# Weight-block sums one half product earlier, and the seven-product stream three half tiles later, in a one-core decoder layer

## The chip, the core and the metric

The kernel runs on one core of a Trainium2 chip. The metric is the device time in microseconds of one execution. Every number of time below is from three timed runs of the kernel before or from one further execution of it under the hardware profiler.

## What is computed

One decoder layer on 256 tokens of width 2048, all in float32. The core of the reference, cut:

```python
proj = x @ w_in
q_a, k_a, v_a, z_a, u_g, v_g, z_g, q_c, z_c, g_logit = jnp.split(proj, split_at, axis=-1)
y_a = _moba_attention(q_a, k_a, v_a) * jax.nn.silu(z_a)
y_g = _spatial_gating(u_g, v_g, w_s, b_s, ln_v_g, ln_v_b) * jax.nn.silu(z_g)
mem_k = mem @ w_mem_k
mem_v = mem @ w_mem_v
y_c = _memory_attention(q_c, mem_k, mem_v) * jax.nn.silu(z_c)
gates = jax.nn.sigmoid(g_logit)
merged = (gates[:, :, 0] * (y_a @ w_branch_attn)
          + gates[:, :, 1] * (y_g @ w_branch_sgu)
          + gates[:, :, 2] * (y_c @ w_branch_mem))
x = _layer_norm(DN_ALPHA * x + merged @ w_out, ln_g, ln_b)
```

## The kernel before

Every operand is kept as two float32r parts, a rounded one (`hi`) and the rest (`lo`), and a product of two float32 matrices is made of three TensorE products: hi by hi, hi by lo, lo by hi. The helper `split` (lines 58 to 60) makes the parts: ScalarE (ACT) copies the source to `hi`, then VectorE (DVE) subtracts it from the source to `lo`. So each weight passes ACT and then DVE before TensorE (PE) can use it.

Two streams of work share the engines.

**The classic stream** works through 112 chunks of weights of 1 MB, each in two halves. `load_chunk` brings chunk 70, say, to the tile `raw70`; `prep_half` splits half 0 to `hi70_0`, `lo70_0` (128x1024); `c_half` hands it to 12 or 16 products. `channel_tile` (16 products a half, alternately 512 and 256 columns wide, lines 187 and 188) makes the projections, and `gated_branch` (12 products of 512 columns, lines 712 to 714) the three branch products. In the order of the program: memory values and keys; zc and qc with the memory attention (`ms`, `mpt`, `mo`); za with branch 2; q and k with eight heads of block attention (`s`, `pt`, `o`); ug with branch 0 (chunks 67 to 74); ug (75 to 79); zg with the spatial gating (`mix`, scales of the tile `vg` on line 663; chunks 80 to 87); branch 1 (88 to 95); the output product. The `hi` and `lo` tiles have 3 buffers each, so a half may be split three halves ahead.

**The seven-product stream** (`s_stream`, lines 327 to 393) makes eight units of 1024 columns (the six gate halves, the attention values and v_g) with seven products of 2x2 blocks instead of eight. A unit has 14 half products, numbered s = 14u + r, two for each of M1, M5, M6, M3, M7, M4, M2 in this order. The weights of unit u come in four blocks with two halves of 1 MB each: the tile `b0_u_h` is B11, `b1` B12, `b2` B22, `b3` B21. M5, M6 and M4 need B11 less another block. These sums are made in place in `b0`, one after another, by `sub` on DVE (128x2048, line 311). A fourth sum, B12 less B22, is made in `b1` in M3.

`s_prep(s)` readies half product s: for M5, M6 and M4 the sum, then the split to `sh<s>` and `sl<s>` (128x2048), then the load of the block whose buffer has just come free. `s_stream` calls `s_prep(s + 2)` behind the 12 products of s. The tag `shl` has 4 buffers, hence two half products of `sh` and `sl`. The block `b3` is loaded behind the split of M3 (`s_load`, line 295) and used by the sum of M4, four half products later; it takes the buffer that the split of M3 frees.

The two streams are interleaved by a loop at the end (lines 776 to 784). After each of the 160 steps of the classic stream behind zc, it takes as many of the 112 half products as keep them in proportion, once `LEAD` steps have passed, so that the last is due `TAIL` steps before the end:

```python
while done_s < S_STEPS and done_s * (C_STEPS - LEAD - TAIL) < (done_c - LEAD) * S_STEPS:
    step(lambda: next(ss))
```

This sets the order in which the program is written down. The framework then arranges the instructions of each engine anew by its own estimate of when each is ready (`schedule_with_timeline_sim=True`), so the order in which the engines get them is not the program's. On the chip each engine takes its list from front to back.

Of the kernel before, what the change touches and what calls it, by code (L numbers as in the profile page):

```python
# [11 lines left out]
ALU = mybir.AluOpType  # L12
# [4 lines left out]
S = 256  # L17
# [10 lines left out]
def decoder_layer(ctx, tc, xT, memT, x_tok, w_st, w_mv, w_mk, w_zc, w_qc, w_za, w_qk, w_ug, w_zg,  # L28
                  w_br, w_o, w_sT, sgu_bc, ln_g, ln_b, out):
    nc = tc.nc  # L30
# [17 lines left out]
    def new_acc(name):  # L48
        return psum.tile([P, 512], F32, tag="acc", name=name, bufs=3)

    def new_sps(name):
        return psum.tile([P, 512], F32, tag="sps", name=name, bufs=3)
# [5 lines left out]
    def split(hi, lo, v):  # L58
        nc.scalar.activation(hi, v, AF.Copy)  # L59
        nc.vector.tensor_tensor(lo, v, hi.bitcast(F32), op=ALU.subtract)  # L60
# [89 lines left out]
    def c_half(ahead=2):  # L150
        while len(ready) < ahead + 1 and ptr["half"] < 2 * len(chunks):
            prep_half()
        return ready.pop(0)
# [31 lines left out]

    def channels_mm(ps, x, hi, lo, first, last):
        nc.tensor.matmul(ps, hi, x, start=first, stop=False)  # L187
        nc.tensor.matmul(ps[:, S:2 * S], lo, x[:, 0:S], start=False, stop=last)

    def channel_tile(xs, name, fin):  # L190

        ps = new_acc(name)
        for h in range(2):
            hi, lo = c_half()
            for k in range(8):
                c = slice(k * P, (k + 1) * P)
                channels_mm(ps, xs(8 * h + k), hi[:, c], lo[:, c], h == 0 and k == 0, h == 1 and k == 7)
            if h == 1:
                def done():
                    fin(ps)  # L200
                    tick()
                late.append(done)
            yield
# [81 lines left out]
    UNITS = 8  # L285
    PRODUCTS = ("M1", "M5", "M6", "M3", "M7", "M4", "M2")
    FORM = {"M5": 1, "M6": 2, "M3": 4, "M7": 3}
    rt, shl, xsf, sp = {}, {}, {}, {}

    def s_load(u, blk, h):  # L290
        if u >= UNITS:
            return
        tag, bufs = ("rA", 2) if blk == 0 else ("rB", 4)
        t = wts.tile([P, 2048], F32, tag=tag, name=f"b{blk}_{u}_{h}", bufs=bufs)
        nc.sync.dma_start(t, w_st[u, blk, h])
        rt[u, blk, h] = t

    B11, B12, B22, B21 = range(4)

    def s_prep(s):  # L300
        u, r = divmod(s, 14)
        if u >= UNITS:
            return
        p, h = divmod(r, 2)
        p = PRODUCTS[p]
        if p in FORM:
            t = wts.tile([P, 4, 2 * P], F32R, tag="xsf", name=f"xf{s}", bufs=3)
            nc.sync.dma_start(t.bitcast(F32), xf_d[FORM[p], h])
            xsf[s] = t
        b = lambda blk: rt[u, blk, h]  # L310
        sub = lambda o, x, y: nc.vector.tensor_tensor(o, x, y, op=ALU.subtract)  # L311
        src = {"M1": B11, "M5": B11, "M6": B11, "M4": B11, "M3": B22, "M7": B12, "M2": B21}[p]
        if p == "M5":
            sub(b(B11), b(B12), b(B11))
        elif p == "M6":
            sub(b(B11), b(B22), b(B11))
        elif p == "M4":
            sub(b(B11), b(B21), b(B11))
        hi = wts.tile([P, 2048], F32R, tag="shl", name=f"sh{s}", bufs=4)
        lo = wts.tile([P, 2048], F32R, tag="shl", name=f"sl{s}", bufs=4)  # L320
        split(hi, lo, b(src))
        shl[s] = (hi, lo)
        if p == "M3":
            sub(b(B12), b(B22), b(B12))
            s_load(u, B21, h)
        elif p == "M7":
            s_load(u + 1, B12, h)
        elif p == "M4":
            s_load(u + 1, B11, h)
        elif p == "M2":  # L330
            s_load(u + 1, B22, h)

    def snap(name):
        return work.tile([P, 512], F32, tag="snap", name=name, bufs=5)

    def s_stream(finish):

        bank, kept = {}, {}

        def keep(name, ps):  # L340
            kept[name] = snap(name)
            nc.scalar.activation(kept[name], ps, AF.Copy)

        def result(u, t, n, ps, name):
            r = kept[name]
            nc.vector.tensor_tensor(r, ps, r, op=ALU.add)
            finish(u, t, n, r)

        def evacuate(u, p):
            if p == "M1":  # L350
                keep(f"k1_{u}", bank["b"])
            elif p == "M5":
                keep(f"k5_{u}", bank["d"])
            elif p == "M6":
                keep(f"k6_{u}", bank["b"])
            elif p == "M3":
                result(u, 0, 1, bank["d"], f"k6_{u}")
            elif p == "M7":
                keep(f"k7_{u}", bank["b"])
                result(u, 1, 1, bank["b"], f"k5_{u}")  # L360
            elif p == "M4":
                result(u, 1, 0, bank["c"], f"k7_{u}")
            else:
                result(u, 0, 0, bank["a"], f"k1_{u}")

        BANK = {"M1": "b", "M6": "b", "M7": "b", "M5": "d", "M3": "d", "M4": "c", "M2": "a"}
        for s in range(14 * UNITS):
            u, r = divmod(s, 14)
            p, h = divmod(r, 2)
            p = PRODUCTS[p]  # L370
            if h == 0 and p in ("M1", "M5", "M4", "M2"):
                bank[BANK[p]] = new_sps(f"s{p}_{u}")
            ps = bank[BANK[p]]
            hi, lo = shl.pop(s)
            for kk in range(4):
                k = 4 * h + kk
                if p in FORM:
                    ah, al = xsf[s][:, kk, 0:P], xsf[s][:, kk, P:2 * P]
                else:
                    k += 0 if p == "M1" else 8  # L380
                    t = P if p == "M4" else 0
                    ah, al = xhl[:, k, t:t + P], xhl[:, k, S + t:S + t + P]
                c = slice(kk * 512, (kk + 1) * 512)
                first = h == 0 and kk == 0 and p in ("M1", "M5", "M4", "M2")
                last = h == 1 and kk == 3
                nc.tensor.matmul(ps, ah, hi[:, c], start=first, stop=False, skip_group_check=True)  # L386
                nc.tensor.matmul(ps, ah, lo[:, c], start=False, stop=False, skip_group_check=True)  # L387
                nc.tensor.matmul(ps, al, hi[:, c], start=False, stop=last, skip_group_check=True)  # L388
            xsf.pop(s, None)
            s_prep(s + 2)  # L390
            if h == 1:
                late.append(lambda u=u, p=p: evacuate(u, p))
            yield
# [76 lines left out]
    while x_work:  # L470
        x_work.pop(0)()
        step(lambda: None)
    s_prep(0)
    s_prep(1)


    yhl = {}
# [281 lines left out]
    def classic():  # L759
        yield from gate_tiles("zc", AF.Silu, szc_d)  # L760
        new_y(2)
        yield from mem_attention()
        yield from gate_tiles("za", AF.Silu, sza_d, range(3))
        yield from gated_branch(2, 0)
        yield from gate_tiles("za", AF.Silu, sza_d, range(3, 8))
        new_y(0)
        yield from block_attention()
        yield from gate_tiles("ug", AF.Gelu_apprx_tanh, gu_d, range(3))
        yield from gated_branch(0, 1)
        yield from gate_tiles("ug", AF.Gelu_apprx_tanh, gu_d, range(3, 8))  # L770
        new_y(1)
        yield from gating()
        yield from gated_branch(1, 2)

    C_STEPS, S_STEPS = 160, 14 * UNITS
    LEAD, TAIL = 2, 14
    cs, ss = classic(), s_stream(s_finish)
    done_c = done_s = 0
    for _ in run(cs):
# [39 lines left out]
    for n in range(3):  # L819
        ps = [new_acc(f"o{n}_{t}") for t in range(2)]  # L820
        for kq in range(8):
            hi, lo = c_half()
# [8 lines left out]
    for t in range(2):  # L831
        for i, c0 in enumerate((1536, 1792)):
            ps = new_sps(f"o{3 + i}_{t}")
# [82 lines left out]
```

## Time and profile before

| | |
|---|---|
| three timed runs | 1009.95, 1011.45, 1011.49 us; median 1011.45 us |
| the profiled execution | 1014.38 us, of it 1012.7 us from its first to its last instruction |
| TensorE's granted clock, mean | 0.99 of full speed |
| DMA | 269.28 MB, 266 GB/s in the mean |

The profiled execution is the one that all rows below come from. It is 2.9 us longer than the median of the timed runs. Busy shares overlap: PE's matmuls are pipelined, and a stretch in which PE is shown busy can still hold fewer products than another of the same length. A lowered clock shows in the granted clock of a stretch.

### The profile page before, as it was taken

What the parts mean: (1) busy time and instruction counts of PE and PEld (TensorE: products, weight loads), DVE (VectorE), ACT (ScalarE), POOL (GpSimd) and SP (SyncE); (2) the same over time, 40 slices, a digit from 0 to 9 for tenths busy, and PEclk for the clock granted to TensorE, in tenths of its full rate; (3) what the DMA queues carried; (4) which work ended last, traced back from release to release, by engine and by line L of the source; (5) the groups of instructions that cost most, each with busy time, mean ns of one, the idle gap of its engine ahead of it and who ended that gap; (6) DMA issues with size and microseconds to landing.
All of it is one profiled execution on the core that took longest, in us unless ns stands there. A gap on an engine that the chain in (4) does not pass through costs nothing.

```text
span 1012.7 us, 12913 instructions
## 1 busy us (share of the span) xinstructions
PE 982.4 (97%) x4888; PEld 826.9 (82%) x4888; DVE 820.6 (81%) x800; ACT 590.6 (58%) x646; POOL 12.0 (1%) x17
## 2 busy tenths in 40 slices
PE   9999899999999999999999999979998999999995
PEld 7788788888888788888888888858877888878885
DVE  5865987898779799888979898899979877676657
ACT  5654665565577566556556566867555559554430
POOL 0000000000000000000000000000000010000000
PEclk9999999999999999999999999989999999999998
DMA  8899589738965897598379648937994785778622
GB/s 330 313 387 414 181 304 348 277 132 296 364 223 168 295 382 278 165 362 346 134 271 356 236 139 281 382 106 269 414 366 147 284 286 183 249 259 303 238 84 83
DMA packets 68126, 269.28 MB, mean 266 GB/s; under 512 B 7521, under 2 KB 21601, under 8 KB 45537
## 3 DMA queue, kind: packets, MB, share of 16 engines
q1 hardware_dynamic: 68064, 268.47, 72.2%
q8 instruction: 38, 0.62, 0.2%
q14 instruction: 24, 0.19, 0.0%
HBM read 245.37 MB, written 23.07 MB: 265 GB/s over the span
## 4 chain that ended last, share of the span: by engine, by line
PE 85%; DVE 5%; ACT 4%; DMA 3%; issue 2%; POOL 0%; SPq 0%; DVEq 0%; ACTq 0%
PE sM L386 9%; PE sM L387 9%; PE sM L388 9%; PE b L713 4%; PE b L714 3%; PE b L712 3%; PE zc L187 3%; PE k L187 3%; PE qc L187 3%; PE za L187 3%; PE q L187 3%; PE mk L187 3%; PE o L800 3%; PE o L799 3%; PE o L798 3%; PE mv L423 3%
## 5 line engine op out<-in xcount | busy, mean ns | idle before, releaser
L59 ACT ACTIVATE hi<-raw 128x1024 fp32r<-128x1024 f32 (+1 forms) x218 | 228.3, 1051 | 191.4 <-PE o L800 29.1
L60 DVE TENSOR_TENSOR lo<-raw,hi 128x1024 fp32r<-128x1024 f32 (+1 forms) x218 | 263.1, 1214 | 77.2 <-ACT hi L59 76.4
L60 DVE TENSOR_TENSOR sl<-b,sh 128x2048 fp32r<-128x2048 f32 x112 | 256.3, 2291 | 57.1 <-ACT sh L59 56.7
L59 ACT ACTIVATE sh<-b 128x2048 fp32r<-128x2048 f32 x112 | 214.4, 1915 | 99.6 <-PE sM L387 89.3
L311 DVE TENSOR_TENSOR b<-b,b 128x2048 f32<-128x2048 f32 x64 | 146.3, 2289 | 8.0 <-DMA b<-in_w_st_dram 7.8
L386 PE MATMUL sM<-sh,xf 128*128 128x512 f32 x256 | 101.3, 396 | 6.5 <-ACT sh L59 6.5
L387 PE MATMUL sM<-sl,xf 128*128 128x512 f32 x256 | 100.6, 393 | 2.5 <-DVE sl L60 2.5
L388 PE MATMUL sM<-sh,xf 128*128 128x512 f32 x256 | 100.2, 391 | 0.0
L387 PE MATMUL sM<-sl,xhl 128*128 128x512 f32 x192 | 76.8, 400 | 0.6 <-DVE sl L60 0.6
L386 PE MATMUL sM<-sh,xhl 128*128 128x512 f32 x192 | 77.4, 403 | 0.0
L713 PE MATMUL b<-lo,yhl 128*128 128x512 f32 x192 | 76.1, 397 | 1.2 <-DVE lo L60 1.2
L388 PE MATMUL sM<-sh,xhl 128*128 128x512 f32 x192 | 76.3, 397 | 0.0
L714 PE MATMUL b<-hi,yhl 128*128 128x512 f32 x192 | 74.9, 394 | 0.0
L712 PE MATMUL b<-hi,yhl 128*128 128x512 f32 x192 | 74.0, 398 | 0.9 <-ACT hi L59 0.9
L386 PEld LDWEIGHTS sM<-sh,xf 128*128 128x128 f32 x256 | 48.3, 189 | 18.3 <-ACT sh L59 7.9
L387 PEld LDWEIGHTS sM<-sl,xf 128*128 128x128 f32 x256 | 48.2, 188 | 12.9 <-DVE sl L60 3.2
L388 PEld LDWEIGHTS sM<-sh,xf 128*128 128x128 f32 x256 | 48.1, 188 | 10.3
L187 PE MATMUL ug<-xhl,hi 128*128 128x512 f32 x128 | 46.3, 400 | 1.5 <-ACT hi L59 1.5
L187 PE MATMUL q<-xhl,hi 128*128 128x512 f32 x128 | 46.5, 399 | 0.0
L187 PE MATMUL qc<-xhl,hi 128*128 128x512 f32 x128 | 46.2, 400 | 0.0
L187 PE MATMUL zc<-xhl,hi 128*128 128x512 f32 x128 | 45.7, 398 | 0.4 <-ACT hi L59 0.4
L187 PE MATMUL k<-xhl,hi 128*128 128x512 f32 x128 | 46.0, 397 | 0.0
(296 smaller groups left out, 1853.1 us busy)
## 6 DMA issues: line engine op xcount, KB each, us to landing
b<-in_w_st_dram SPq DMA_DIRECT2D x64, 1024.0 KB, 7.2
xf<-xf SPq DMA_DIRECT2D x64, 512.0 KB, 6.0
raw<-in_w_br_dram SPq DMA_DIRECT2D x24, 1024.0 KB, 6.8
raw<-in_w_qk_dram SPq DMA_DIRECT2D x16, 1024.0 KB, 7.3
raw<-in_w_o_dram SPq DMA_DIRECT2D x16, 1024.0 KB, 5.4
raw<-in_w_mk_dram SPq DMA_DIRECT2D x8, 1024.0 KB, 10.1
raw<-in_w_zc_dram SPq DMA_DIRECT2D x8, 1024.0 KB, 6.5
raw<-in_w_qc_dram SPq DMA_DIRECT2D x8, 1024.0 KB, 7.6
```

Of the source, the lines that this page charges most:

```text
L59: nc.scalar.activation(hi, v, AF.Copy)
L60: nc.vector.tensor_tensor(lo, v, hi.bitcast(F32), op=ALU.subtract)
L187: nc.tensor.matmul(ps, hi, x, start=first, stop=False)
L311: sub = lambda o, x, y: nc.vector.tensor_tensor(o, x, y, op=ALU.subtract)
L386: nc.tensor.matmul(ps, ah, hi[:, c], start=first, stop=False, skip_group_check=True)
L387: nc.tensor.matmul(ps, ah, lo[:, c], start=False, stop=False, skip_group_check=True)
L388: nc.tensor.matmul(ps, al, hi[:, c], start=False, stop=last, skip_group_check=True)
L423: nc.tensor.matmul(ps[t][n], lhs, rhs[:, n * 512:(n + 1) * 512], start=(k == 0 and rhs is hi and lhs is xh[t]), stop=(k == KT - 1 and lhs ...
L712: nc.tensor.matmul(ps[t], yh, hi[:, c], start=(k == 0), stop=False)
L713: nc.tensor.matmul(ps[t], yh, lo[:, c], start=False, stop=False)
L714: nc.tensor.matmul(ps[t], yl, hi[:, c], start=False, stop=(k == 7))
L798: nc.tensor.matmul(ps[:, 0:n], mh, hi, start=first, stop=False)
```

## The change

The three sums of M5, M6 and M4 leave `s_prep` for a function `s_sum`, which `s_stream` calls with s + 3 just ahead of `s_prep(s + 2)`. So in the program the sum stands one half product ahead of its split. The first one is called with 2 behind `s_prep(1)`. The sum of M3 stays in `s_prep`. LEAD goes from 2 to 5 and TAIL from 14 to 11: the proportion of the two streams between is unchanged (144 steps to 112 half products), and every half product is written three steps of the classic stream later. (`channels_mm` now returns its last product; nothing uses it.)

```diff
+    def s_sum(s):
+
+        u, r = divmod(s, 14)
+        if u >= UNITS:
+            return
+        p, h = divmod(r, 2)
+        other = {"M5": B12, "M6": B22, "M4": B21}.get(PRODUCTS[p])
+        if other is not None:
+            o = rt[u, B11, h]
+            nc.vector.tensor_tensor(o, rt[u, other, h], o, op=ALU.subtract)
+
     def s_prep(s):
...
         src = {"M1": B11, "M5": B11, "M6": B11, "M4": B11, "M3": B22, "M7": B12, "M2": B21}[p]
-        if p == "M5":
-            sub(b(B11), b(B12), b(B11))
-        elif p == "M6":
-            sub(b(B11), b(B22), b(B11))
-        elif p == "M4":
-            sub(b(B11), b(B21), b(B11))
         hi = wts.tile([P, 2048], F32R, tag="shl", name=f"sh{s}", bufs=4)
...
             xsf.pop(s, None)
+            s_sum(s + 3)
             s_prep(s + 2)
...
     s_prep(0)
     s_prep(1)
+    s_sum(2)
...
     C_STEPS, S_STEPS = 160, 14 * UNITS
-    LEAD, TAIL = 2, 14
+    LEAD, TAIL = 5, 11
```

What it does to the engines' lists is shown at three places. In the names the first number is that of the half product (`sh84`, `sl84`), of the chunk and half (`hi70_0`), or of the unit and half (`b0_6_1`); the last number counts tiles and means nothing.

**Place 1: ACT where unit six begins (its first half product is 84).** Before:

```order
L59 ACTIVATE sh84_5606<-b0_6_0_5425 128x2048
L599 ACTIVATE ptT7_5303<-pt7_5299 128x384
L704 ACT_TABLE_LOAD
L704 ACTIVATE sg000_5382<-sg000_5382 128x512
L59 ACTIVATE sh85_5638<-b0_6_1_5462 128x2048
L704 ACTIVATE sg010_5385<-sg010_5385 128x512
L704 ACTIVATE sg001_5523<-sg001_5523 128x512
L753 ACTIVATE vg_5405<-k1_5_5039 128x512
L704 ACTIVATE sg011_5526<-sg011_5526 128x512
L59 ACTIVATE sh86_5720<-b0_6_0_5425 128x2048
L635 ACT_TABLE_LOAD
L635 ACTIVATE vg_5405<-vg_5405 128x512
```

and now, from half product 82 on:

```order
L59 ACTIVATE sh82_5567<-b3_5_0_5281 128x2048
L711 ACT_TABLE_LOAD
L711 ACTIVATE sg000_5340<-sg000_5340 128x512
L711 ACTIVATE sg010_5343<-sg010_5343 128x512
L760 ACTIVATE vg_5459<-k5_5_5228 128x512
L642 ACT_TABLE_LOAD
L642 ACTIVATE vg_5459<-vg_5459 128x512
L59 ACTIVATE sh83_5619<-b3_5_1_5325 128x2048
L59 ACTIVATE hi70_0_5496<-raw70_5389 128x1024
L760 ACTIVATE vg_5459<-k7_5_5550 128x512
L711 ACT_TABLE_LOAD
L711 ACTIVATE sg001_5490<-sg001_5490 128x512
```

Before, the last head (`ptT7`) and the first sigmoids of branch 0 (`sg`) fall between `sh84` and `sh86`, and no chunk is split there: `hi70_0` follows only on `sh87`. Now they fall between `sh82` and `sh84`, and the chunks of branch 0 (`hi70_0`, `hi70_1`, `hi71_0`) alternate with `sh83`, `sh84`, `sh85`. Six instructions stand between `sh82` and `sh83`.

**Place 2: DVE from the split of half product 34 (the first of M3 in unit two) to the sum of M4, which takes `b3_2_0`.** Before:

```order
L60 TENSOR_TENSOR sl34_2869<-b2_2_0_2418,sh34_2868 128x2048
L60 TENSOR_TENSOR lo39_1_2913<-raw39_2773,hi39_1_2912 128x1024
L726 TENSOR_TENSOR sg201_2810<-b2_10_2808,sg201_2810 128x512
L60 TENSOR_TENSOR sl35_2906<-b2_2_1_2511,sh35_2905 128x2048
L726 TENSOR_TENSOR sg211_2813<-b2_11_2809,sg211_2813 128x512
L311 TENSOR_TENSOR b0_2_0_2319<-b3_2_0_2873,b0_2_0_2319 128x2048
L60 TENSOR_TENSOR lo40_0_2963<-raw40_2840,hi40_0_2962 128x1024
```

and now:

```order
L60 TENSOR_TENSOR sl34_2929<-b2_2_0_2515,sh34_2928 128x2048
L60 TENSOR_TENSOR lo40_1_2938<-raw40_2798,hi40_1_2937 128x1024
L60 TENSOR_TENSOR lo41_0_2977<-raw41_2872,hi41_0_2976 128x1024
L60 TENSOR_TENSOR lo41_1_3015<-raw41_2872,hi41_1_3014 128x1024
L309 TENSOR_TENSOR b0_2_0_2399<-b3_2_0_2933,b0_2_0_2399 128x2048
L60 TENSOR_TENSOR sl35_2970<-b2_2_1_2594,sh35_2969 128x2048
```

The sum has come ahead of `sl35`, which now waits behind it.

**Place 3: DVE where unit seven begins, from the split of half product 99 to that of 100.** Before:

```order
L60 TENSOR_TENSOR sl99_6364<-b0_7_1_6164,sh99_6363 128x2048
L311 TENSOR_TENSOR b0_7_0_6122<-b1_7_0_6002,b0_7_0_6122 128x2048
L311 TENSOR_TENSOR b0_7_1_6164<-b1_7_1_6075,b0_7_1_6164 128x2048
L60 TENSOR_TENSOR lo77_0_6084<-raw77_5968,hi77_0_6083 128x1024
L663 TENSOR_TENSOR vg_5405<-vg_5405,sc1_6494 128x2x128
L663 TENSOR_TENSOR vg_5405<-vg_5405,sc2_6601 128x2x128
L60 TENSOR_TENSOR lo77_1_6126<-raw77_5968,hi77_1_6125 128x1024
L208 TENSOR_TENSOR ug4_6166<-ug4_6082,ug4l_6167 128x256
L311 TENSOR_TENSOR b1_7_0_6002<-b2_7_0_6213,b1_7_0_6002 128x2048
L663 TENSOR_TENSOR vg_5405<-vg_5405,sc3_6690 128x2x128
L60 TENSOR_TENSOR sl100_6442<-b0_7_0_6122,sh100_6441 128x2048
```

and now:

```order
L60 TENSOR_TENSOR sl99_6444<-b0_7_1_6240,sh99_6443 128x2048
L60 TENSOR_TENSOR lo82_0_6463<-raw82_6318,hi82_0_6462 128x1024
L60 TENSOR_TENSOR lo82_1_6484<-raw82_6318,hi82_1_6483 128x1024
L208 TENSOR_TENSOR zg1_6528<-zg1_6461,zg1l_6529 128x256
L309 TENSOR_TENSOR b0_7_1_6240<-b1_7_1_6151,b0_7_1_6240 128x2048
L678 TENSOR_TENSOR m0_6536<-mix0_6533,sc0_6360 128x256
L60 TENSOR_TENSOR lo83_0_6551<-raw83_6412,hi83_0_6550 128x1024
L60 TENSOR_TENSOR sl100_6523<-b0_7_0_6194,sh100_6522 128x2048
```

Unit seven stood beside chunks 76 to 79 and the scales of `vg`, and now stands beside chunks 81 to 84; three sums stood between the two splits, and one does now.

## Rows read from the trace of the kernel before

**Rows 1.** The page, part 1: busy time, share of the span, instructions.
```profile
PE 982.4 (97%) x4888; PEld 826.9 (82%) x4888; DVE 820.6 (81%) x800; ACT 590.6 (58%) x646; POOL 12.0 (1%) x17
```

**Rows 2.** Whom PE waited for: us in total, times, longest us.
```profile
PE sM L386 <- ACT sh L59: 6.5, 3, 2.8
PE sM L387 <- DVE sl L60: 3.1, 3, 1.8
PE mix L668 <- POOL ws L657: 1.8, 1, 1.8
PE b L713 <- DVE lo L60: 1.2, 2, 0.8
```

**Rows 3.** Busy us by stretch (x instructions): PE, PEld, DVE, ACT, POOL; clock, DMA share, GB/s.
```profile
75.00:100.00 25.00, 25.00 (x146) 21.86 (x145) 13.29 (x14) 11.90 (x14) 0.00 (x0) 1.00 1.02 418
325.00:350.00 25.00, 25.00 (x112) 20.69 (x111) 18.26 (x14) 15.93 (x15) 0.00 (x0) 1.00 0.78 272
...
655.00:694.00 39.00, 33.80 (x127) 26.07 (x126) 38.02 (x34) 27.67 (x29) 0.00 (x0) 0.87 0.44 150
...
745.00:790.00 45.00, 39.17 (x200) 32.29 (x199) 44.55 (x39) 26.02 (x28) 3.45 (x1) 1.00 0.59 210
```

**Rows 4.** The same columns, two short stretches inside the first loss.
```profile
668.00:672.00 4.00, 4.00 (x12) 3.12 (x12) 4.00 (x3) 1.90 (x3) 0.00 (x0) 0.58 0.00 0
679.00:686.00 7.00, 6.81 (x16) 5.02 (x17) 7.00 (x8) 1.70 (x3) 0.00 (x0) 0.52 0.00 0
```

**Rows 5.** DVE in order of time: start us, us, line, operation.
```profile
665.01 2.29 DVE L60 TENSOR_TENSOR sl<-b,sh 128x2048 fp32r<-128x2048 f32 x1
667.21 2.29 DVE L311 TENSOR_TENSOR b<-b,b 128x2048 f32<-128x2048 f32 x1
669.41 2.29 DVE L60 TENSOR_TENSOR sl<-b,sh 128x2048 fp32r<-128x2048 f32 x1
...
679.27 1.24 DVE L726 TENSOR_TENSOR sg<-b,sg 128x512 f32<-128x512 f32 x2
680.42 2.29 DVE L60 TENSOR_TENSOR sl<-b,sh 128x2048 fp32r<-128x2048 f32 x1
...
689.43 2.36 DVE L60 TENSOR_TENSOR lo<-raw,hi 128x1024 fp32r<-128x1024 f32 x2
691.70 0.17 DVE L217 RECIPROCAL vgr<-vgr 128x2 f32<-128x2 f32 x1
```

**Rows 6.** ACT in order of time, the same columns.
```profile
660.04 1.28 ACT L704 ACT_TABLE_LOAD   x1
...
661.87 1.90 ACT L59 ACTIVATE sh<-b 128x2048 fp32r<-128x2048 f32 x1
663.68 1.14 ACT L704 ACTIVATE sg<-sg 128x512 f32<-128x512 f32 x2
```

**Rows 7.** DVE at the sum of M4 in unit two, in order of time.
```profile
339.12 2.29 DVE L60 TENSOR_TENSOR sl<-b,sh 128x2048 fp32r<-128x2048 f32 x1 [3.71 <-ACT sh L59]
...
348.98 2.29 DVE L311 TENSOR_TENSOR b<-b,b 128x2048 f32<-128x2048 f32 x1 [3.03 <-DMA b<-in_w_st_dram]
351.19 1.22 DVE L60 TENSOR_TENSOR lo<-raw,hi 128x1024 fp32r<-128x1024 f32 x1
```

**Rows 8.** The DMA queue (SP) there: start of the issue.
```profile
341.44 0.33 SPq L295 DMA_DIRECT2D b<-in_w_st_dram  x1
```

**Rows 9.** Line 311 (all sums): DVE's idle time ahead of it, us and times, and what ended it.
```profile
  DMA b<-in_w_st_dram: 7.8, 4
```

**Rows 10.** The page, part 6: loads of blocks, KB each, median us to landing.
```profile
b<-in_w_st_dram SPq DMA_DIRECT2D x64, 1024.0 KB, 7.2
```

**Rows 11.** A split of unit five on DVE, and the first product that takes it.
```profile
619.18 2.28 DVE L60 TENSOR_TENSOR sl<-b,sh 128x2048 fp32r<-128x2048 f32 x1
...
627.49 0.40 PE L387 MATMUL sM<-sl,xf 128*128 128x512 f32 x1
```

**Rows 12.** The chain that ended last, in order of time: start us, us, what.
```profile
859.69 4.41 DMA gl<-k
...
878.21 5.39 DMA sg<-gl
```

More of the change, by code (lines that the diff above doesn't have):

```diff
@@ L187, in channels_mm @@
         nc.tensor.matmul(ps, hi, x, start=first, stop=False)
-        nc.tensor.matmul(ps[:, S:2 * S], lo, x[:, 0:S], start=False, stop=last)
+        return nc.tensor.matmul(ps[:, S:2 * S], lo, x[:, 0:S], start=False, stop=last)
     def channel_tile(xs, name, fin):
```

## The prediction

> **What bounds the kernel now.** Four views, in this order. The page's first part gives TensorE (PE) 982.4 us of 1012.7, 97%, and DVE 820.6 [rows 1]: PE is the engine to look at, and what can be won lies in the places where it runs short. The view of whom PE waited for [rows 2] names them: the split of the seven-product stream on ACT (`sh`, 6.5 us, one wait of 2.8), the same on DVE (`sl`, 3.1 us), once `mix` on POOL (1.8 us), twice a `lo` (1.2 us). Short waits hide here, and so do products that start late while PE counts as busy, so the third view is products per stretch [rows 3]. Where nothing holds PE back, 112 products of 512 columns take 25 us, 0.223 us each; the channel tiles with their alternating widths take 25/146 = 0.171 us. From 655 to 694, 127 products should take 28.3 us and take 39.0: **10.7 us are lost**, with DVE busy for 38.02 of 39.0, PE's granted clock 0.87 and DMA at 0.44. Within it are 668 to 672 with clock 0.58 and 679 to 686 with 0.52 [rows 4], near the lower of the two levels, 1.2 GHz, after PE had run short of weights. From 745 to 790 PE idles for 45.00 - 39.17 = **5.8 us**, and DVE is busy for 44.55 of 45. So DVE, idle for a fifth of the span, is the bound in these two stretches, where units six and seven start. The fourth view, DVE's instructions in time [rows 5], gives prices as start to start: a split or a sum of 128x2048 2.20 us, the split of a half chunk 2.27/2 = 1.13, a 128x512 operation 1.15/2 = 0.57. On ACT [rows 6]: `sh` 1.81, a 128x512 activation 0.57, a table load 1.28.
>
> The cause in both stretches: a half product is 12 products, 2.7 us of PE, and in M5, M6 and M4 it takes 4.4 us of DVE (sum and split). Beside classic halves (2.7 us of PE for 1.13 us of DVE) this averages out; where half products stand back to back, or extra DVE work joins them, it doesn't.
>
> **The change, part by part.**
>
> *The sums' new place.* The number of operations stays the same, so DVE keeps its 820.6 us. The framework arranges the lists anew, and in the order 52 of the 64 sums stand behind the same split as before. What acts is therefore mainly the shift of the two streams against each other. The returned last product costs nothing (no instruction). The first hundred or so rows of DVE's list are the same, so I put the start of the stream at 0.
>
> *Unit six (place 1).* Before, half products 84 to 87 ran almost alone: between `sl84` and `sl87` DVE had 8 large operations, 17.6 us, and 3.2 of small ones, 20.8 in all, for 57 products, 12.7 us: 8.1 short. Now chunks of branch 0 alternate with them: 8 large (17.6), 6 `lo` (6.8), 8 small (4.6), 29.0 us, for 101 products, 22.5 us: 6.5 short. A lead of splits over products covers some of it: `sl77`, in unit five, ends 6.0 us ahead of its product [rows 11]. The shortfall of before came through in full, with 2.6 more from ACT and the rest; so I let 2 be covered and 4.5 remain (ends 0.5 and 6.5). On ACT, between `sh82` and `sh83`, there are two table loads and four activations, 4.8 us, and then `sh83`, 1.8: 6.6 against two halves of PE, 5.4, 1.2 short (0 to 2.8, the longest such wait now). For the collision of the last head with the unit's first blocks I allow 1.8 (0 to 2.8). Sum 7.5 for 10.7: **-3.2** (ends -10.2 and +1.4).
>
> *Unit seven (place 3).* Three sums stood between `sl99` and `sl100`, now one, and the scales of `vg` are gone from there. From `sl98` to `sl101` DVE has 7 large (15.4), 3 `lo` (3.4) and 2 us of small ones, 20.8 us as before, but PE now has 36 products of 512 columns and 50 of channels, 8.0 + 8.6 + 0.7 of mixing = 17.3 for 14.0. 3.5 us short, which a lead of 6.0 covers. `mix` now comes some 12 halves behind the issue of what it waited for; that wait goes. 0.5 of 5.8 remains: **-5.3** (-5.8 to -2.8, if half of the shortfall and the `mix` wait stay).
>
> *The wait on b3 (place 2).* The load of `b3` is issued when the split of M3 ends, 339.12 + 2.29, at 341.44 [rows 7, 8]; the sum of M4 waits 3.03 us for it, starts at 348.98, and the next `lo` only behind it, at 351.19 [rows 7]. All such waits come to 7.8 us in 4 places [rows 9], and the median load takes 7.2 [rows 10]. Now 3 `lo`, 3.4 us, stand between `sl34` and the sum, where 4.5 us stood: the wait becomes about 4.1, and `sl35` stands behind it. It ends 7.5 + 2.2 + 2.2 = 11.9 us after `sl34`, while PE has 34 products, 7.6 us; 4.3 short less a lead of 0.4 to 3: 2.2, of which before had 0.7. **+1.5** (0 to +3.2).
>
> *Behind unit six.* DVE's list stays full into unit seven, so a stall is put off rather than paid once: **+1.5** (0 to +3).
>
> *The end.* The chain of the end goes through the gate's store to DRAM and its reload, 4.41 and 5.39 us [rows 12], and three steps later in the order it lies nearer to its use. **+0.5** (0 to +5.4, one reload).
>
> *Sum:* -3.2 - 5.3 + 1.5 + 1.5 + 0.5 = **-5.0**. The profiled execution took 1014.38 us and would take 1009.4; it stands 2.9 above the median of the timed runs, 1011.45, so for the median I say **1006.4**.
>
> **The rivals.**
>
> *Both stalls vanish.* If the alternation at unit six lets the lead of 6.0 us [rows 11] cover the 6.5 there, PE doesn't run dry and the clock stays at 1.00: -10.7 - 5.8 + 3.5 = -13.0, **998.4**. For it: of 10.7 us, much was products at a lowered clock [rows 4], which go with the cause. Against: the lead must have been built by then, and DVE is loaded from the head before. 0.12.
>
> *The shift only moves the shortfall.* DVE's work is the same, the sums hardly moved, and what was short in unit six turns up in units six and seven: the sum of the gains is paid back, **1011.5**, within 0.2% (2 us, about what a measurement of this kernel tells from no change). For it: DVE full for 38.02 of 39 and 44.55 of 45 us [rows 3], and six us still short. Against: over the span DVE is idle for a fifth [rows 1], so there is room around these stretches to work ahead. This is also the case in which the change doesn't do what it says. 0.16.
>
> *Slower: DVE's list blocks on a load.* A sum of M4 that comes earlier stands earlier in front of a load that doesn't. DVE takes its list in order: at 351.19 a `lo` whose source was ready began only behind the sum that had waited 3.03 us [rows 7]. Counting for all 16 such sums the work between the split of M3 and the sum, the shortfall to 7.2 us was 25.3 in all and is now 33.5: +8.2 us of waits, with splits `sl35`, `sl63` and `sl77` now behind them. It decides wherever the lead of the splits is below the wait, as around `sl34`; where it is 6.0, as at `sl77`, the wait is free. If all 8.2 come through, and half of unit six's gain falls away, -1.6 - 5.3 + 8.2 + 1.5 + 0.5 = +3.3: **1014.8**. The Trainium skill, "PSUM — Partial Sum Buffer", section "Engine vs sequencer instructions", calls the queues of ScalarE, VectorE and GpSimdE strictly first in, first out; by that rule a sum put earlier can only add to the wait of what follows it, and the trace agrees at the one place shown, 351.19. Against this rival: the four waits now total 7.8 us, and PE's waits for `sl` and `lo` together only 4.3 [rows 2, 9]. 0.18.
>
> **How the numbers follow.** Forecast 0.54, both stalls vanish 0.12, moved 0.16, slower 0.18. The range goes from 998.5, where the second case is centred, to 1014.5, just short of the centre of the last; half of each lies outside, 0.15. The forecast's own range, from its unknowns of about 3 us each way, is 1002.5 to 1010. Faster by over 0.2%: 0.54 + 0.12 = 0.66; the same 0.16; slower 0.18.
>
> **What would show it.** Up to the first 117 us nothing should differ. Where unit six starts, right is: about 7 us lost instead of 10.7, a clock above 0.87, and `hi70_0` beside `sh83`. Where unit seven starts: DVE still near 100%, PE idle by less than 1 us, no wait of `mix` on POOL. At the sum of `b0_2_0`: an idle time of 4 us for a DMA, `sl35` behind it, and PE short by some 2 us. DVE's idle time on loads of blocks should grow from 7.8 us toward 10 to 16. The forecast is wrong if PE has a clock near 0.5 in unit six for as long as now, if a new stretch with full DVE and idle PE appears behind unit seven, or if PE's wait for `sl` grows beyond the 3.1 us of now in units two to five, which would be the last rival.

## The result, and the profile after

Five timed runs of the changed kernel give a median of 1004.72 us (1002.88 to 1006.71) beside 1011.45 us: a ratio of 0.9936, 95% interval 0.9918 to 0.9955, so 6.7 us faster; 5.0 were forecast, 1006.4 us. The profiled execution took 1006.01 us (span 1004.3), 1.3 us above its median, and is 8.4 us shorter than the one of before.

The page's part 1 of the changed kernel:

```profile
PE 979.5 (98%) x4888; PEld 824.4 (82%) x4888; DVE 819.6 (82%) x800; ACT 590.5 (59%) x647; POOL 13.2 (1%) x17
```

Against [rows 1] the work is the same and the span shorter. Whom PE waited for (us in total, times, longest):

```profile
PE sM L391 <- ACT sh L59: 4.4, 2, 2.8
PE sM L392 <- DVE sl L60: 2.6, 1, 2.6
PE b L720 <- DVE lo L60: 1.6, 3, 0.8
```

Of the lines of [rows 2], `mix` on POOL is gone. Busy time by stretch, columns as in [rows 3], changed kernel:

```profile
655.00:694.00 39.00, 36.87 (x157) 28.68 (x156) 35.85 (x33) 32.71 (x32) 0.00 (x0) 1.00 0.71 257
694.00:745.00 51.00, 48.04 (x233) 39.54 (x232) 48.40 (x54) 30.09 (x30) 0.00 (x0) 1.00 0.86 310
745.00:790.00 45.00, 45.00 (x234) 38.19 (x233) 40.46 (x31) 30.12 (x30) 3.29 (x3) 1.00 0.81 317
```

and the second of them in the kernel before:

```profile
694.00:745.00 51.00, 51.00 (x234) 42.30 (x232) 43.36 (x40) 28.69 (x24) 0.00 (x0) 1.00 0.98 390
```

From 655 to 694 PE now makes 157 products instead of 127, at a granted clock of 1.00 instead of 0.87; 157 x 0.223 = 35.0 us, so 4.0 are lost where 10.7 were. From 745 to 790 it no longer idles, where 5.8 us were lost. Between the two a new idle time of 3.0 us has appeared.

The whole span can be set out in this way: for each product the time from its start to the next one's, less the median of this time over all products of the same line, tiles and shape; what exceeds 0.06 us is summed. It gives PE's lost time in us. The third and fourth rows are two runs told of below, sums_only and shift_only; all five engines' lists are those of the kernel before in the one, and those of the changed kernel in the other, so that each set of lists is seen in two executions:

| | start to 130 | 130 to 640 | 640 to 694 | 694 to 740 | 740 to 800 | behind 800 | all |
|---|---|---|---|---|---|---|---|
| before | 10.5 | 5.9 | 11.7 | 0.0 | 7.0 | 2.3 | 37.3 |
| changed | 12.5 | 5.7 | 3.9 | 3.8 | 0.2 | 2.8 | 28.9 |
| lists of before (sums_only) | 10.8 | 5.1 | 9.1 | 0.6 | 8.4 | 1.0 | 35.0 |
| changed lists (shift_only) | 9.5 | 5.5 | 4.3 | 4.5 | 0.2 | 0.9 | 24.9 |

From before to changed the sum fell by 8.4 us, the difference of the two spans. The start, whose list did not change, differs by 2.0; the same lists lost 9.5 there in shift_only, so that much is scatter between executions. The other pair shows what is more than scatter: from 740 to 800 the loss goes from 7.0 and 8.4 us to 0.2 in both, while from 640 to 740 it goes from 11.7 and 9.7 to 7.7 and 8.8, so by 4.0 in one pair and by 0.9 in the other. Most of the gain that holds is unit seven's. The lowered clock varies likewise: with the same lists the granted clock from 655 to 694 was 0.87 in the kernel before and 0.96 in sums_only.

DVE in order of time behind unit six's start, changed kernel, and the longest of PE's waits there:

```profile
692.43 2.28 DVE L309 TENSOR_TENSOR b<-b,b 128x2048 f32<-128x2048 f32 x1
694.63 1.22 DVE L60 TENSOR_TENSOR lo<-raw,hi 128x1024 fp32r<-128x1024 f32 x1
695.77 2.28 DVE L322 TENSOR_TENSOR b<-b,b 128x2048 f32<-128x2048 f32 x1
697.97 0.16 DVE L215 TENSOR_SCALAR vgv<-vmv 128x2 f32<-128x2 f32 x1
698.04 2.28 DVE L60 TENSOR_TENSOR sl<-b,sh 128x2048 fp32r<-128x2048 f32 x1
```

```profile
700.38 0.50 PE L392 MATMUL sM<-sl,xf 128*128 128x512 f32 x1 [2.59 <-DVE sl L60]
```

The split at 698.04 is `sl87`. The two sums ahead of it are for half products 88 (M6) and 93 (M7); they stand first in DVE's list, and PE waits 2.59 us for the split behind them.

### The profile page after: what moved, and what is told of

Read it like the earlier page. It is cut to its first block, busy times and chain, and to the rows that moved or that the text cites. A ratio compares the mean times of both kernels' runs of the same rounds, so it can differ in the third digit from the quotient of the medians.

```text
span 1004.3 us, 12911 instructions
## 1 busy us (share of the span) xinstructions
PE 979.5 (98%) x4888; PEld 824.4 (82%) x4888; DVE 819.6 (82%) x800; ACT 590.5 (59%) x647; POOL 13.2 (1%) x17
## 4 chain that ended last, share of the span: by engine, by line
PE 79%; DVE 9%; DMA 6%; issue 3%; ACT 3%; SPq 0%; DVEq 0%; ACTq 0%
PE sM L391 8%; PE sM L392 8%; PE sM L393 8%; PE za L187 3%; PE k L187 3%; PE q L187 3%; PE zg L187 3%; PE qc L187 3%; PE mk L187 3%; PE mv L429 3%; PE o L806 3%; PE o L807 3%; PE o L805 3%; PE zc L187 3%; PE b L720 2%
## 5 line engine op out<-in xcount | busy, mean ns | idle before, releaser
L309 DVE TENSOR_TENSOR b<-b,b 128x2048 f32<-128x2048 f32 x48 | 109.5, 2283 | 15.3 <-DMA b<-in_w_st_dram 15.3
L187 PE MATMUL za<-xhl,hi 128*128 128x512 f32 x128 | 46.2, 400 | 0.0
```

The costliest lines, as they stand in the source:

```text
L309: nc.vector.tensor_tensor(o, rt[u, other, h], o, op=ALU.subtract)
```

## Experiments

"Before" in each is the median of the kernel before, measured beside it.

### Which half of the change acts

sums_only, the changed kernel but for

```diff
-    LEAD, TAIL = 5, 11
+    LEAD, TAIL = 2, 14
```

> The kernel before with the sums written one half product ahead of their split, and the two streams in the proportion of before (LEAD 2, TAIL 14). Theory (only the shift acts): the lists of all five engines are those of the kernel before row for row, so the time is that of before within 0.2% (1009.4 to 1013.5 us) and PE again loses some 10 us from 655 to 694 and 6 us from 745 to 790. Rival (the sums' place brings part of it): faster by 1 to 5 us.

1012.17 us, before 1012.47; ratio 0.9997 (0.9988 to 1.0007). shift_only, the kernel before but for

```diff
-    LEAD, TAIL = 2, 14
+    LEAD, TAIL = 5, 11
```

> The kernel before with LEAD 5 and TAIL 11, the sums left directly ahead of their splits. Theory (only the shift acts): the lists of all five engines are those of the changed kernel, so the time is that of the changed kernel, 1004.7 us within 2 us, and the profile's places of loss are its places. Rival (the sums' place brings part of it): slower than the changed kernel by 1 to 5 us.

1003.56 us, before 1012.47; ratio 0.9919 (0.9906 to 0.9932), the changed kernel's 0.9936 within scatter. With line and tile numbers left out, the lists of all five engines of sums_only are those of the kernel before, row for row, and those of shift_only are the changed kernel's. So the framework undoes the move of the sums altogether, and the change is its two numbers.

### Is it DVE's work that bounds the two stretches?

nosums6 and nosums7 are the kernel before, with the three pairs of sums of one unit left out, here those of unit six (7 stands for 6 in nosums7):

```diff
-        if p == "M5":
+        if u == 6:
+            pass
+        elif p == "M5":
```

> The kernel before without the six sums of M5, M6 and M4 in unit six (its products use B11 as it is). 13.2 us of DVE are gone; half products 81 to 86 still stand back to back as before. Theory (DVE's work bounds the start of unit six): of the 10.7 us lost from 655 to 694 at most 4 remain, what ACT's list and the last head leave, the granted clock stays above 0.95 there, and the median falls by 5 to 9 us, to 1002 to 1006. Rival (the last head and ACT's list hold it up, and the products at a lowered clock follow from that): 7 us or more remain, and the median falls by less than 3 us.

> The kernel before without the six sums of M5, M6 and M4 in unit seven (its products use B11 as it is). Theory (DVE's work bounds the start of unit seven): PE's idle time from 745 to 790, 5.8 us, falls to 2 us or less, the wait of mix on POOL among what may remain, and the median falls by 3 to 6 us, to 1005.5 to 1008.5. Rival (the stall comes from loads of blocks or from ACT's list, and DVE is only busy beside it): 4 us or more remain.

nosums6: 1000.45 us, ratio 0.9888 (0.9873 to 0.9904). nosums7: 1005.97 us, ratio 0.9938 (0.9925 to 0.9951). The stretches of [rows 3], nosums6:

```profile
655.00:694.00 39.00, 36.56 (x156) 29.59 (x155) 36.68 (x39) 34.31 (x34) 0.00 (x0) 0.96 0.62 220
...
745.00:790.00 45.00, 43.82 (x231) 37.19 (x230) 40.19 (x32) 25.27 (x28) 4.03 (x3) 1.00 0.58 214
```

and nosums7:

```profile
655.00:694.00 39.00, 33.78 (x127) 26.07 (x126) 36.51 (x31) 27.72 (x30) 0.00 (x0) 0.87 0.44 146
...
745.00:790.00 45.00, 44.75 (x235) 38.27 (x236) 39.94 (x38) 28.13 (x29) 0.29 (x1) 1.00 0.67 251
```

In nosums7 unit six stays as it was, product for product, and unit seven's idle time falls from 5.8 to 0.25 us, the wait of `mix` included. In nosums6, 39 - 156 x 0.223 = 4.2 us remain, where at most 4 were expected. By the account above, 6.0 us were lost from 676 to 686 in the kernel before, and they are gone; of the 4.3 lost from 662 to 672, 3.75 remain. So that part of unit six's loss is not its sums'. It begins with the kernel before's longest wait there, for `sh86`, while ACT worked without a gap, the sigmoids `sg` ahead of that split:

```profile
667.71 0.50 PE L386 MATMUL sM<-sh,xf 128*128 128x512 f32 x1 [2.38 <-ACT sh L59]
```

The granted clock of 0.58 from 668 to 672 [rows 4] follows on this wait. nosums6's median fell by 12.0 us where 5 to 9 were expected: unit seven came to stand one to two chunks later in its list, and most of that stall went too (5.8 to 1.2 us). In nosums7 too the framework arranged unit seven anew, half products more evenly between the chunks. So the two runs show that the stalls from 676 to 686 and in unit seven go when the unit's sums go, but not how much of this is DVE's shorter work and how much the new order.

### One step less, one step more

The edit of lead4, in the changed kernel; lead6 has 6, 10 in its place:

```diff
-    LEAD, TAIL = 5, 11
+    LEAD, TAIL = 4, 12
```

> The changed kernel with LEAD 4 and TAIL 12, so shifted by two steps instead of three. In its list branch 0's chunks come one and a half half products later into unit six than in the changed kernel (69 behind half product 84, not 82), and unit seven stands beside chunks 78 to 83. Between half products 84 and 87 DVE has about as much PE work beside it as in the changed kernel. Theory (what counts is how much PE work stands beside a unit's first sums): most of the gain is there, 1003 to 1009 us, with 3 to 6 us lost from 655 to 700 and under 3 us from 745 to 800. Rival (three steps meet a lucky alignment of loads, or the gain comes from the end): 1010 us or more.

> The changed kernel with LEAD 6 and TAIL 10, one step further. From half product 82 to 90 its list is that of the changed kernel; the last head comes two half products earlier; unit seven moves on to chunks 82 to 86. Theory: the same time as the changed kernel or up to 3 us less, 1001 to 1006 us, as the loss of 1.9 us at the last head shrinks; the loss on a split of branch 0 behind unit six, 3.3 us in the changed kernel near 697, stays. Rival (every step later costs at the end, where the gate's store and reload come nearer to their use): 1007 us or more, with over 4 us lost behind 885.

lead4: 1018.91 us, ratio **1.0072** (1.0050 to 1.0093). lead6: 1015.89 us over nine runs from 1011.97 to 1017.57, ratio **1.0031** (1.0012 to 1.0050). Both expectations failed: a step either way turns a gain of 7 us into a loss. By the account above, lead4 loses 10.8 us from 651 to 694 and 9.5 from 770 to 800; lead6 loses 12.8 from 645 to 705 and 7.1 from 811 to 821. For lead6 the rival named the end, but only 0.4 us were lost behind 885. In both the longest wait is that of `mix` on POOL. lead4, whom PE waited for:

```profile
PE mix L675 <- POOL ws L664: 6.4, 1, 6.4
```

The masking of `ws` in lead4, GpSimd and then DVE in order of time:

```profile
778.17 6.99 POOL L664 TENSOR_SCALAR_AFFINE_SELECT ws<-ws 128x128 f32<-128x128 f32 x2 [775.99 <-DMA gu<-gu]
```

```profile
777.67 2.29 DVE L60 TENSOR_TENSOR sl<-b,sh 128x2048 fp32r<-128x2048 f32 x1
779.88 0.42 DVE L670 TENSOR_TENSOR vg<-vg,sc 128x256 f32<-128x256 f32 x1
780.21 2.35 DVE L60 TENSOR_TENSOR lo<-raw,hi 128x1024 fp32r<-128x1024 f32 x2
782.48 2.28 DVE L309 TENSOR_TENSOR b<-b,b 128x2048 f32<-128x2048 f32 x1
784.68 0.42 DVE L208 TENSOR_TENSOR ug<-ug,ug7l 128x256 f32<-128x256 f32 x1
```

The POOL row holds two masks, the first of 6.75 us, the second of 0.29. The first ends at 784.92, just behind the start of the first DVE operation that has an operand in PSUM (`ug`); the five before it take two operands from SBUF without a gap. In the kernel before, the mask at 782.31 took 3.45 us and ended likewise 0.26 us into such an operation; 21 of the 80 masks of the ten kernels with the masks on GpSimd took 0.29, the longest 10.82 (pool_m3, below).

tri2, tri4, tri5 and tri6 have LEAD 2, 4, 5 and 6, and the mask on DVE:

```diff
+    tri = const.tile([P, P], F32, name="tri")
+    nc.gpsimd.memset(tri, 1.0)
+    nc.gpsimd.affine_select(out=tri, in_=tri, compare_op=ALU.is_ge, fill=0.0, base=0, pattern=[[1, P]],
+                            channel_multiplier=-1)
...
-            nc.gpsimd.affine_select(out=st["w"], in_=st["w"], compare_op=ALU.is_ge,
-                                    fill=0.0, base=0, pattern=[[1, P]], channel_multiplier=-1)
+            nc.vector.tensor_tensor(st["w"], st["w"], tri, op=ALU.mult)
```

> The kernel of lead4 with the masking of ws (its upper triangle) done on DVE with a constant 0/1 tile, not on GpSimd; nothing else is written differently. In lead4 the first mask began at 778.17, when its load had landed, took 6.75 us in which DVE ran without a gap, and mix waited 6.4 us for it; other masks take 0.29 us. Theory (GpSimd's mask is held up by DVE's back-to-back work, and that is most of what lead4 lost against the changed kernel in unit seven): the wait of mix falls under 1 us, the loss from 770 to 800 from 9.5 to under 3 us, and the median from 1018.9 to between 1010 and 1014. Rival (the mask only reports a late load): mix waits as long for the load, and the median stays at 1017 or more.

> The changed kernel with the masking of ws done on DVE with a constant 0/1 tile. There mix does not wait, its first mask had begun at 766.4, 15.5 us ahead of use. Theory: no gain, eight operations of 0.2 us on DVE beside other work; 1003 to 1007 us. Rival (the masks on GpSimd also hold DVE up while they wait): 1 to 3 us faster than the changed kernel.

> The kernel of lead6 with the masking of ws done on DVE with a constant 0/1 tile. In lead6 a mask at 810.81 took 6.01 us beside a full DVE and mix waited 5.1 us. Theory (held up by DVE): that wait goes, 5 to 7 us are won, the median falls from 1015.9 to between 1008 and 1011.5. Rival: the median stays within 3 us of 1015.9.

> The streams of the kernel before (LEAD 2, TAIL 14, list of the engines as before but for a few places near the masks) with the masking of ws on DVE with a constant 0/1 tile. It splits the gain of the shift in unit seven: in the kernel before, a mask took 3.45 us on GpSimd at 782.31 and mix cost 2.2 us there. Theory (the mask is only that part, the rest of the shift's gain is DVE's work in units six and seven): 1.5 to 3.5 us faster than before, 1008.5 to 1010.5 us, with some 3 us still lost on splits near 766 to 772 and 10 us from 655 to 694. Rival (the held mask explains the gain of the shift as it explained most of what lead4 and lead6 lost): 1003.5 to 1006.5 us. Second rival (mix only waits for its load): no faster than before by more than 1 us.

| LEAD | mask on GpSimd | mask on DVE |
|---|---|---|
| 2 | the kernel before | 1011.01 us, 0.9988 (0.9977 to 1.0000) |
| 4 | 1018.91 us, 1.0072 (1.0050 to 1.0093) | 1007.48 us, 0.9954 (0.9939 to 0.9969) |
| 5 | 1004.72 us, 0.9936 (0.9918 to 0.9955) | 1004.68 us, 0.9926 (0.9911 to 0.9940) |
| 6 | 1015.89 us, 1.0031 (1.0012 to 1.0050) | 1005.27 us, 0.9928 (0.9911 to 0.9946) |

With the mask on DVE, lead4 and lead6 gain 11 us each, more than expected, and the wait of `mix` is gone in all four; by the account 7.2 us of it (770 to 800) and 7.1 (811 to 821) are at that wait. tri5 came out as expected. With that wait gone, the shift gives 3.5 us at LEAD 4 and some 6 at 5 and 6 against tri2, by the ratios: no cliff a step either way, though LEAD 4 gives about half of what 5 and 6 do. But the mask is not ready earlier. DVE in tri4 at the same place:

```profile
784.37 0.41 DVE L208 TENSOR_TENSOR ug<-ug,ug7l 128x256 f32<-128x256 f32 x1
784.71 0.28 DVE L669 TENSOR_TENSOR ws<-ws,tri 128x128 f32<-128x128 f32 x1
```

It ends at 784.99, in lead4 at 784.92. What changed is PE's list: the first `mix` stands 43 rows later in it (it starts at 787.8, other products run before it). The likely reason, which no run shows, is that the framework reckoned the mask on GpSimd as done soon. For tri2, 1.5 to 3.5 us were expected; PE's busy time from 745 to 790 rose from 39.17 to 41.37 us, 2.2 as worked out, but the median fell by 0.75 us only, with an interval of 0 to 2.3 us. The rival in which the mask explains the shift's gain is out.

### A load made later, and sums on GpSimd

b3late changes the changed kernel so:

```diff
+        if s - 1 in hold_b2:
+            nc.gpsimd.tensor_tensor(tiny, hold_b2.pop(s - 1)[:, 0:1], lo[:, 0:1].bitcast(F32), op=ALU.subtract)
+            s_load(u, B21, (s - 1) % 2)
...
             sub(b(B12), b(B22), b(B12))
-            s_load(u, B21, h)
+            hold_b2[s] = b(B22)
```

> The changed kernel with the load of b3 held back by one half product (a read of one column of b2 on GpSimd, which also takes the next split, holds the buffer). Test of the rival in which DVE's list blocks on this load. Rival (a wait of a sum of M4 reaches PE): DVE's idle time on loads of blocks grows from 15.3 us by 3 to 5 us for most of the 16 sums, to 40 us or more, and the median rises by 8 us or more, to 1012 or above. Theory (the splits' lead of 4 us or more over their products covers it): the idle time grows to 25 us or more and the median stays within 4 us of the changed kernel, 1003 to 1008 us.

1004.92 us, ratio 0.9937 (0.9916 to 0.9959): no cost. But the premise failed. The load in unit two was issued 8.5 us behind the end of `sl34` (at 353.86 us) instead of at its end, yet DVE's idle time on loads of blocks fell, from 15.3 to 10.8 us: the framework put the sum behind more work, `sl35` and `sl36` among it. The run says nothing on what a longer wait would cost.

pool_m3 moves the sums of M3 (16 of the 64) off DVE:

```diff
-            sub(b(B12), b(B22), b(B12))
+            nc.gpsimd.tensor_tensor(b(B12), b(B22), b(B12), op=ALU.subtract)
```

> The changed kernel with the sixteen sums of M3 (B12 less B22) on GpSimd instead of DVE, all other sums as they were; 35 us of work leave DVE. Theory (what is left at units six and seven is DVE's list, which takes sums of later half products ahead of a split that PE waits for): the 3.3 us near 697 vanish, DVE has under 790 us, and the median falls by 2 to 6 us, to 998.5 to 1003. Rival (GpSimd takes so long for one, over 12 us, or slows DVE beside it, that M7 waits for its sum): 1006 us or more, with PE waiting for GpSimd.

1036.87 us, ratio 1.0243 (1.0222 to 1.0265). One sum takes GpSimd 4.6 us, well under the 12 of the rival, but it stops DVE. GpSimd and DVE in unit two, in order of time:

```profile
319.08 4.62 POOL L329 TENSOR_TENSOR b<-b,b 128x2048 f32<-128x2048 f32 x1 [91.16 <-DVE b L309]
```

```profile
318.87 0.68 DVE L351 TENSOR_TENSOR k<-sM,k 128x512 f32<-128x512 f32 x1
319.47 6.38 DVE L60 TENSOR_TENSOR sl<-b,sh 128x2048 fp32r<-128x2048 f32 x1
325.77 1.21 DVE L60 TENSOR_TENSOR lo<-raw,hi 128x1024 fp32r<-128x1024 f32 x1
```

The split takes 6.38 us instead of 2.28 and ends 2.2 us behind GpSimd's sum, as if it had begun when that ended; `k`, which has an operand in PSUM, takes its usual 0.68 beside it. DVE has 16 operations of 2.2 us less, which would be 784, and is busy for 847.1 us: some 62 us held up, 3.9 for each sum, and PE waits 18.3 us for splits instead of 2.6. Each of the 16 sums has one operation of DVE beside it that is lengthened in this way, by 61 us in all over their usual times. So the rival was right that it would be slower and that GpSimd slows DVE; PE waited for DVE's splits, though, and not for GpSimd.

## Why the prediction was right, point by point

**That only the shift acts** was more right than said: the prediction counted 52 of the 64 sums behind the same split as before and took the shift as what mainly acts. The other 12 moved with the shift; without it, in sums_only, not one sum moved.

**Unit six**, forecast 7.5 us left of 10.7, showed 4.0. **Behind it**, forecast 1.5, it showed 3.0, of which 2.59 are the wait for `sl87`. Together 9.0 were forecast and 7.0 measured, a gain of 3.7 where 1.7 was forecast; by the account the two executions with the changed lists gained 4.0 and 0.9 from 640 to 740, so the size is not settled. Direction and place were right. The cause, DVE's work, is borne out for the 6.0 us from 676 to 686 alone (nosums6); the 4.3 from 662 to 672 begin with a wait for ACT, where the prediction had 2.6 for ACT and the rest. Two terms were mis-sized. ACT and the last head, 1.2 and 1.8 us, came to 1.9 in all, near 662. DVE's 4.5 and 1.5 us came to some 5, and most of it later than said: in the changed kernel the splits of half products 84 to 87 ended 1.9, 0.5, 0.4 and 0.05 us ahead of their first products. So the lead was used up step by step, and the shortfall came out beyond 690.

**Unit seven**, forecast -5.3, gave -5.8, and by the account -6.7 from 740 on, since a wait of 1.5 us for a `hi`, just ahead of the stretch that the prediction counted, went too. The lead covered the shortfall, as forecast: `sl98` to `sl101` ended 7.3, 3.1, 4.6 and 4.8 us ahead of their products, where `sl100` and `sl101` had led by 0.05. DVE was busy for 40.46 of the 45 us, though, and not near 100%, as the sign had it. nosums7 agrees with the cause as stated, DVE's work. But the wait of `mix` was no matter of its load alone, as the text had it. In the changed kernel it goes because the first mask, at 766.38, comes 15 us ahead of its use; at LEAD 4 and 6 it came back, at 6.4 and 5.1 us, and made these kernels slower than before. No rival named this, though [rows 2] names POOL: a slower outcome one step away stood in the row of the `mix` wait.

**The wait on b3** failed as a step: +1.5 us was forecast for unit two, and PE lost nothing more there. DVE and the DMA queue, changed kernel:

```profile
345.19 2.29 DVE L60 TENSOR_TENSOR sl<-b,sh 128x2048 fp32r<-128x2048 f32 x1 [0.71 <-ACT sh L59]
...
352.30 2.29 DVE L309 TENSOR_TENSOR b<-b,b 128x2048 f32<-128x2048 f32 x1 [1.07 <-DMA b<-in_w_st_dram]
354.51 2.28 DVE L60 TENSOR_TENSOR sl<-b,sh 128x2048 fp32r<-128x2048 f32 x1
```

```profile
347.51 0.33 SPq L295 DMA_DIRECT2D b<-in_w_st_dram  x1
```

The order was as read, `sl35` behind the sum. But the load landed 4.8 us after its issue, not 7.5 as in the kernel before, so the sum waited 1.07 us instead of 4.1. The 7.5 was that one execution's: with the same lists, sums_only issued the load at 341.89, and the sum began at 346.78, 4.9 us later:

```profile
346.78 2.29 DVE L309 TENSOR_TENSOR b<-b,b 128x2048 f32<-128x2048 f32 x1 [0.39 <-DMA b<-in_w_st_dram]
```

And `sl34` led its product by 4.4 us where it had led by 0.7: the lead was taken from the kernel before, as if the shift left it alone. DVE's idle time on block loads did double, as forecast:

```profile
DVE b L309 <- DMA b<-in_w_st_dram: 15.3, 11, 3.2
```

against 7.8 us in 4 places [rows 9], and in the other pair it went from 4.1 to 16.4. (Beside `sl35`, `sl63` and `sl77`, `sl91` too came to stand behind its sum.) PE lost no more for it: 5.7 us from 130 to 640, after 5.9. So the rival in which DVE's list blocks on a load had its waits, but not its price.

**The end**, forecast +0.5, gave +0.5 in the account (2.3 to 2.8), which is scatter: in the other pair it went from 1.0 to 0.9. No run shows this term. **The start** was 0 within its scatter. Of the rivals, the shortfall that only moves came true in part, with the 3.0 us behind unit six; the stalls that both vanish did for unit seven.

**The sum** of -5.0 came near the -6.7 of the medians partly by luck. In the profiled executions the terms missed by -3.5 (unit six), +1.5 (behind it), some -1.7 (b3) and -0.5 or more (unit seven), and these spans differ by 8.4 us. The term that carries the result, unit seven's, was right in cause and nearly in size.

What stays open: why lead4, lead6, tri4 and tri6 lose 10.3 to 12.8 us from 645 to 705, about what the lists of before lose there (9.7 and 11.7), where the lists of the changed kernel lose 7.1 and 8.8 and tri5 9.1, though PE's list there is much alike. In lead6 one wait was ACT's: `sh88` stood behind a sigmoid that waited 3.71 us for the reload of a gate half. No run tells whether that is the whole of it.

No run that makes the whole layer beats the changed kernel clearly: shift_only and tri5 take its time (0.9919 and 0.9926). tri5 is the safer form, as its neighbours at LEAD 4 and 6 stay within 3 us of it.

## What to carry to other kernels

Where a scheduler arranges the lists, compare them before believing an edit: half of this one was undone to the last row, and the other half worked by moving stretches in which one engine was full to places with more work for another, in unit seven beyond doubt. Take two executions of the same lists before giving a microsecond of one trace a cause: here the time of one load (7.5 and 4.9 us), a loss at the end (2.3 and 1.0) and 2 us of a stall changed between them. A gain that rests on such an alignment should be tried one step to each side. And a small operation on GpSimd that PE waits for is a risk where DVE is full, whatever its own 0.29 us.

## What the runs showed of the hardware

GpSimd and DVE kept each other out. A sum of two SBUF tiles on GpSimd (4.6 us) held a DVE split with two SBUF operands until its end (6.38 us instead of 2.28) and let operations with a PSUM operand pass (0.68 us). The other way round, GpSimd's mask of 0.29 us took 6.75 us in lead4 while DVE ran two-operand work from SBUF without a gap. This fits what the Trainium skill says in "SBUF — State Buffer", section "SBUF: two separate sides": the port pair that the two engines share is an exclusive lock, held by an operation of either for its whole length, on DVE's side by one with two SBUF inputs. The page gives it to whoever starts first.

Which of the two goes next while one waits differed from case to case. In lead4, DVE's next operation came ahead of the waiting mask four times running. But of the 53 masks that took longer than 0.35 us, 45 got in as soon as the operation then on DVE ended, 32 of them ahead of an operation with two SBUF operands, which then took some 0.09 us longer than usual. The changed kernel's first mask did, ending at 766.95, and the `lo` beside it took 1.31 us where 1.22 is usual:

```profile
766.38 0.57 POOL L664 TENSOR_SCALAR_AFFINE_SELECT ws<-ws 128x128 f32<-128x128 f32 x1 [764.22 <-DMA b<-in_w_st_dram]
```

```profile
764.51 2.29 DVE L60 TENSOR_TENSOR sl<-b,sh 128x2048 fp32r<-128x2048 f32 x1 [0.52 <-ACT sh L59]
766.72 1.31 DVE L60 TENSOR_TENSOR lo<-raw,hi 128x1024 fp32r<-128x1024 f32 x1
```

So a wait as long as lead4's is the exception, and no run tells what brings it about.
